# Attention part of a streaming encoder step: ScalarE and VectorE in written order, steps divided otherwise, weights split three chunks ahead

## The chip, the cores and the metric

One core of one Trainium2 chip runs the whole program. The metric is device time in microseconds (us) of one execution; the kernel before has a median of 2910.96 us over 3 runs (2910.06 to 2913.39).

## The reference, cut to what matters

One step of a two-layer encoder over 512 new frames ("prompt") and 8 running streams of 16 frames each ("sample"), 640 token columns in all; the model width is 2048.

```
# layer A
z = rmsnorm(x, norm_a) @ w_in_a ; u, gate = z[:4096], z[4096:]
x = x + (pool_mix(u) * silu(gate)) @ w_out_a
# shared keys, values, forget logits
kvf = rmsnorm(x, norm_kv) @ w_kv            # K 16 heads x 128, V 16 x 128, 16 logits
logf = log_sigmoid(kvf[..., 4096:] + b_f) ; F = cumsum(logf)
# layer B, 16 heads
z = rmsnorm(x, norm_b) @ w_in_b ; q, gate = z[:2048], z[2048:]
s = q.k / sqrt(128) + F[t] - F[s], causal   # sample streams also see 256 cached rows
o = softmax(s) @ v
x = x + (o * silu(gate)) @ w_out_b
y = rmsnorm(x, norm_f)
```

Everything is in float32. The kernel keeps the precision by splitting an operand into a rounded part (`hi`, type float32r, made on ScalarE) and the rest (`lo = x - hi`, made on VectorE), and by three matmuls for one product: hi*hi, hi*lo, lo*hi.

## The kernel before

**Layers A and K/V.** `pair8` multiplies a 256-column pair of weights by the stream with seven products of 2x2 blocks (m1 to m7, `ORDER`), each in a PSUM bank of its own (banks 0 to 6). `combine` (line 277) builds the four output blocks from them: first `v = m1` is copied out of PSUM by ScalarE (line 289), then VectorE adds and subtracts the others. The next pair's first matmul writes the same bank 0 again. It is called 47 times: 31 pairs of layer A, 16 of K/V. TensorE runs in the order in which the program is written; VectorE, ScalarE, GpSimd and the DMA queue on SyncE are ordered by a planner, which fills a list for each engine ahead of time. On the chip each engine works through its list in order and waits at each instruction for what that needs.

**Forget logits.** `forget_sums(c)` (line 782) adds, for each pair of stream blocks, small matmuls into banks 6 and 7. The last one, `forget_sums(7)`, runs in `last_rows` inside the first K/V pair, and both banks are then copied to `lt` (lines 865 and 866). Bank 7 is also the bank of `norm_stream`'s matmul (line 877), which comes three products later.

**Attention.** For each head `h`, `q_block(h)` and `gate_block(h)` each run `proj`: 16 k-steps of 6 matmuls (`mm3`, line 1069), in 4 chunks of 4 k-steps. At the start of a chunk `chunk()` calls `split_next` (line 1093): the weights of a later chunk are scaled on VectorE (line 1090), rounded on ScalarE (`whi`, line 1098), and the rest is taken on VectorE (`wlo`, line 1100); then `fetchb` asks for another chunk's DMA. `prime` splits two chunks in advance, and `whi` and `wlo` have three buffers each.

Between k-steps, at 9 of the 16 (k-steps 0, 2, 4, 6, 8, 9, 11, 13, 15), `tick()` runs one step of the generator `attn`, up to its next `yield`. In the steady state one head's attention steps are spread over `gate_block(h)` (9 ticks) and `q_block(h+1)` (9 ticks); it has 17 steps. The steps that matter here:

- steps 1, 2, 4, 5: `turn_keys`, VectorE transposes of cached keys into `kct` (line 1232);
- step 3 and step 7: `running`, matmuls of `kct` with the sample queries (line 1237);
- `new(t)`, t = 0 to 3 (steps 3, 6, 8, 9): scores of a 128-query block on TensorE; on VectorE add of F (line 1251), mask (1253), maximum (1255); on ScalarE Exp with a row sum (1257); on VectorE reciprocal (1258) and scaling (1259);
- step 7 also has the same chain for the sample rows, `s2` (lines 1305 to 1315);
- `turn_new(t)` (steps 8, 10, 11, 14): TensorE transposes of the probabilities into a bank from `tbank()`, which alternates between banks 6 and 7; ScalarE copies the rounded part out (`pth`, line 1269), VectorE takes the rest (`ptl`, line 1270);
- steps 12 and 13: transposes of `s2` (four blocks, then one) into the same two banks, copied out by ScalarE (line 1338);
- step 15 and 16: sample output `po` (line 1347); step 17: prompt output `op` (lines 1360 to 1363), ScalarE copies of both into `og`, VectorE product with the gate (line 1371).

After `q_block`'s last k-step VectorE makes `qt` and `qs` from PSUM (lines 1187 to 1190), ScalarE and VectorE split `qt`. After `gate_block`'s last k-step VectorE scales the gate (line 1199) and ScalarE applies Silu (line 1200). ScalarE loads a table whenever it goes from Exp to Silu or back.

**Output projection.** Planned freely on all engines, TensorE included, with `mmx` (line 1413).

## Time and profile before

| | |
|---|---|
| profiled execution | 2911.26 us, of which the span from the first to the last instruction is 2909.3 us |
| median of the runs | 2910.96 us |
| TensorE (PE) busy | 2780.2 us, 96% of the span |
| VectorE (DVE) busy | 2014.5 us, 69% |
| ScalarE (ACT) busy | 1149.5 us, 40% |
| GpSimd (POOL) busy | 382.2 us, 13% |
| layers A and K/V | from the start to about 1956 us |
| attention, 16 heads | about 1961 to 2680 us |
| output projection | from about 2663 us to the end |

TensorE is what the time is made of: where it runs without a gap, only fewer matmuls would help, and where it has gaps, the question is which instruction of another engine ended the gap. A row of the timeline has start, duration, engine, line, operation, output and inputs, and in brackets the idle time before it and what ended that. A row of the view of waits has the total, the number and the longest of such gaps.

### The profile page before, as it was taken

How to read it: one execution, taken by the hardware profiler on the slowest of the kernel's cores; microseconds unless marked ns; L12 is line 12 of the kernel's file. 1: busy time of each engine (PE TensorE's matmuls, PEld its weight loads, DVE VectorE, ACT ScalarE, POOL GpSimd, SP SyncE). 2: the span in 40 equal slices, each digit the busy share in tenths (PEclk: the TensorE clock that was granted, in tenths of full speed). 3: DMA queues.
4: the chain of work that ended last, by engine and by line, in shares of the span. 5: the costliest groups of instructions: out<-in, count | busy, mean ns of one | idle time of the engine just before them, and what ended most of it. 6: DMA issues, size and time to landing. Idle time of an engine off the chain costs nothing. (4 is left out here: it accounts for less than half of the span.)

```text
span 2909.3 us, 46312 instructions
## 1 busy us (share of the span) xinstructions
PE 2780.2 (96%) x18194; PEld 2651.2 (91%) x18194; DVE 2014.5 (69%) x3430; ACT 1149.5 (40%) x1911; POOL 382.2 (13%) x357
## 2 busy tenths in 40 slices
PE   7899999999999999999998999998999999999998
PEld 6799999999999999999998999987888888888787
DVE  7877778887786858584567888875665665656434
ACT  5433333333233435353345555542433433435222
POOL 2112131322420111112023111110000000000000
PEclk8999999999999999999999999999999999999999
DMA  3344444444345877779443554556555554545923
GB/s 124 114 130 134 132 124 129 128 131 125 112 130 164 200 166 182 171 180 182 139 145 89 117 127 117 121 123 152 138 129 128 134 131 118 133 126 110 144 85 110
DMA packets 646755, 390.69 MB, mean 134 GB/s; under 512 B 322756, under 2 KB 601716, under 8 KB 646408
## 3 DMA queue, kind: packets, MB, share of 16 engines
q1 hardware_dynamic: 626952, 333.99, 43.4%
q0 software_dynamic: 19584, 53.75, 8.6%
q8 instruction: 142, 2.33, 0.3%
q14 instruction: 77, 0.63, 0.1%
HBM read 299.66 MB, written 87.99 MB: 133 GB/s over the span
## 5 line engine op out<-in xcount | busy, mean ns | idle before, releaser
L251 PE MATMUL banks<-b,wh 128*128 128x320 f32 x2688 | 602.7, 311 | 16.7 <-ACT cve L289 10.6
L251 PE MATMUL banks<-th,wh 128*128 128x320 f32 x1792 | 566.9, 316 | 9.5 <-DVE cu L293 4.6
L251 PE MATMUL banks<-th,wl 128*128 128x320 f32 x1792 | 557.3, 311 | 2.8 <-DVE wl L84 2.8
L251 PE MATMUL banks<-tl,wh 128*128 128x320 f32 x1792 | 557.6, 311 | 0.7 <-DVE tl L84 0.7
L251 PEld LDWEIGHTS banks<-b,wh 128*128 128x128 f32 x2688 | 452.5, 189 | 18.3 <-ACT cve L289 11.6
L251 PE MATMUL banks<-b,wl 128*128 128x320 f32 x1344 | 417.2, 310 | 0.0
L84 DVE TENSOR_TENSOR wl<-raw,wh 128x768 fp32r<-128x768 f32 (+1 forms) x264 | 308.5, 1170 | 143.0 <-ACT wh L81 139.7
L81 ACT ACTIVATE wh<-sums 128x1024 fp32r<-128x1024 f32 x224 | 236.3, 1055 | 371.0 <-DVE sums L220 370.8
L81 ACT ACTIVATE wh<-raw 128x768 fp32r<-128x768 f32 (+1 forms) x264 | 230.2, 873 | 345.3 <-issue 154.8
L251 PEld LDWEIGHTS banks<-th,wh 128*128 128x128 f32 x1792 | 340.2, 190 | 19.8 <-DVE cu L293 9.1
L1069 PE MATMUL banks<-b,whi 128*128 128x320 f32 x1536 | 358.0, 317 | 0.0
L251 PEld LDWEIGHTS banks<-th,wl 128*128 128x128 f32 x1792 | 339.9, 190 | 3.3 <-DVE wl L84 3.3
L251 PEld LDWEIGHTS banks<-tl,wh 128*128 128x128 f32 x1792 | 340.2, 190 | 1.2 <-DVE tl L84 0.9
L84 DVE TENSOR_TENSOR wl<-sums,wh 128x1024 fp32r<-128x1024 f32 x224 | 282.1, 1259 | 70.6 <-ACT wh L81 70.0
L1069 PEld LDWEIGHTS banks<-b,whi 128*128 128x128 f32 x1536 | 257.8, 191 | 1.2 <-issue 0.4
L251 PEld LDWEIGHTS banks<-b,wl 128*128 128x128 f32 x1344 | 254.1, 189 | 0.0
L1069 PE MATMUL banks<-b,wlo 128*128 128x320 f32 x768 | 197.7, 312 | 0.0
L217 DVE TENSOR_TENSOR sums<-raw 128x512 f32<-128x512 f32 x236 | 174.9, 741 | 11.5 <-POOL sq L769 4.5
L1098 ACT ACTIVATE whi<-raw 128x512 fp32r<-128x512 f32 x144 | 88.9, 628 | 160.7 <-DVE raw L1090 89.8
L1100 DVE TENSOR_TENSOR wlo<-raw,whi 128x512 fp32r<-128x512 f32 x144 | 98.1, 687 | 72.6 <-ACT whi L1098 72.3
L213 ACT ACTIVATE raw<-raw,cols 128x256 f32<-128x256 f32 x256 | 111.1, 497 | 62.1 <-DMA raw<-in_w_kv 62.1
L1069 PEld LDWEIGHTS banks<-b,wlo 128*128 128x128 f32 x768 | 135.4, 190 | 0.0
(395 smaller groups left out, 4864.7 us busy)
## 6 DMA issues: line engine op xcount, KB each, us to landing
raw<-in_w_in_a SPq DMA_DIRECT2D x128, 512.0 KB, 4.0
raw<-in_w_out_a SPq DMA_DIRECT2D x64, 512.0 KB, 5.0
raw<-in_w_kv SPq DMA_DIRECT2D x64, 512.0 KB, 4.1
raw<-in_w_in_b SPq DMA_DIRECT2D x128, 256.0 KB, 3.9
raw<-in_w_grp_a SPq DMA_DIRECT2D x32, 512.0 KB, 5.6
kc<-in_cache_k SPq DMA_DIRECT2D x64, 256.0 KB, 5.3
vc<-in_cache_v SPq DMA_DIRECT2D x16, 1024.0 KB, 5.6
raw<-in_w_out_b SPq DMA_DIRECT2D x64, 256.0 KB, 3.3
```

The costliest lines, as they stand in the source:

```text
L81: a = nc.scalar.activation(hi, x, AF.Copy)
L84: nc.vector.tensor_tensor(lo, x, hi.bitcast(F32), op=ALU.subtract)
L213: nc.scalar.activation(raw[:, k, :], raw[:, k, :], AF.Copy, scale=loads[n][2][:, k : k + 1])
L217: nc.vector.tensor_tensor(sums[:, :, 0:2, :], raw[:, :, 1:3, :], raw[:, :, 0:1, :].to_broadcast([P, 2, 2, P]), op=ALU.subtract)
L251: nc.tensor.matmul(bank[:, :HALF], w[kk][:, a, :], x, start=first and q == 0, stop=last and q == 2)
L1069: nc.tensor.matmul(acc_[:, s, :HALF], w, stream(k, q, s), start=f, stop=l)
L1098: nc.scalar.activation(hi, raw, AF.Copy)
L1100: nc.vector.tensor_tensor(lo, raw, hi.bitcast(F32), op=ALU.subtract)
```

## The change

1. `combine`'s copy of the first product is done by VectorE instead of ScalarE (47 copies).
2. The partial forget logits of banks 6 and 7 are copied to `lt` before the K/V pairs; the last pair's matmuls go to bank 7, one half of the columns at product 2 and one at product 5 of the first K/V pair, and each half is added to `lt` by VectorE. `last_rows` is called at product 5 instead of 2.
3. `whi` and `wlo` have four buffers instead of three, and `prime` splits three chunks in advance. `prime` and the load of `R` stand ahead of the attention part's other loads.
4. From `prime` to the end of the attention part VectorE and ScalarE run in the order in which the program is written, as TensorE does, instead of the planner's.
5. The steps of `attn` are divided otherwise: the scaling of the probabilities (`even`) and the rest of their split (`low`) are taken out of `new` and `turn_new` and written one to three steps later; the values are split in step 8; the new keys of the next head two steps later; and there is one `yield` more, so that a head has 18 steps, one for each tick, and its last step (`op`, line 1360 on) now comes at the last k-step of `q_block`.

The diff, cut to its core:

```diff
         v, u, e = cvue
-        nc.scalar.activation(v, pp["m1"][:, :HALF], AF.Copy)
+        nc.vector.tensor_copy(v, pp["m1"][:, :HALF])
...
+    nc.scalar.activation(lt[:, :HALF], banks[:, 6, :HALF], AF.Copy)
+    nc.vector.tensor_copy(lt[:, HALF:], banks[:, 7, :HALF])
+    def last_forget(n):
+        hs = slice(n * HALF, (n + 1) * HALF)
+        for k in (14, 15):
+            q = k % 4
+            nc.tensor.matmul(banks[32 * q : 32 * q + 32, 7, :HALF], wr[0][:, k * H : k * H + 32], stage[7][:, k % 2, hs],
+                             start=True, stop=True)
+        nc.vector.tensor_tensor(lt[64:, hs], lt[64:, hs], banks[64:, 7, :HALF], op=ALU.add)
     def last_rows():
-        forget_sums(7)
-        nc.scalar.activation(lt[:, :HALF], banks[:, 6, :HALF], AF.Copy)
-        nc.vector.tensor_copy(lt[:, HALF:], banks[:, 7, :HALF])
...
-            if (n, s, j) == (0, 0, 2):
-                last_rows()
+            if (n, s) == (0, 0) and j in (2, 5):
+                last_forget(j // 3)
+                if j == 5:
+                    last_rows()
...
-            hi, lo = (wp.tile([P, 512], F32R, tag=q, name=q, bufs=3) for q in ("whi", "wlo"))
+            hi, lo = (wp.tile([P, 512], F32R, tag=q, name=q, bufs=4) for q in ("whi", "wlo"))
...
+        for _ in range(3):          # prime
+            split_next()
+            fetchb()
...
+    fast.enter_context(tc.manual_schedule(engines={mybir.EngineType.DVE, mybir.EngineType.Activation}))
+    prime()
...
                 nc.scalar.activation(s, s, AF.Exp, bias=mx, accum_out=rw)      # new(t)
-                nc.vector.reciprocal(rw, rw)
-                nc.vector.tensor_scalar_mul(s, s, rw)
+                rws[t] = rw
+            def even(t):
+                nc.vector.reciprocal(rws[t], rws[t])
+                nc.vector.tensor_scalar_mul(pr[t], pr[t], rws[t])
...
+            def low(t):
+                n = min(t + 1, 3)
+                ts = slice(t * P, (t + 1) * P)
+                nc.vector.tensor_tensor(ptl[:, :n, ts], turned[t], pth[:, :n, ts].bitcast(F32), op=ALU.subtract)
...
             turn_keys(kct, 1, 0)
+            even(0)
             yield
...
             running(ss, kct, 1)
+            even(1)                 # ahead of s2's chain
...
             yield
             new(2)
+            nc.vector.reciprocal(rw2, rw2)
+            nc.vector.tensor_scalar_mul(s2, s2, rw2)
+            split_new_values(h)
+            yield
             turn_new(0)
+            even(2)
             yield
+            low(0)
             new(3)
-                split_new_keys(h + 1)
             yield
             turn_new(1)
+            even(3)
+                split_new_keys(h + 1)
             yield
+            low(1)
             turn_new(2)
             yield
+            low(2)
             for js in ((0, 1, 2, 3), (4,)):
...
             turn_new(3)
             yield
+            low(3)
```

## The prediction

> **What bounds the kernel now.** I read the page first, then the time by stage, then TensorE's waits in the two parts that the change touches, then the timelines of VectorE and ScalarE inside one head.

> ```profile
> PE 2780.2 (96%) x18194; PEld 2651.2 (91%) x18194; DVE 2014.5 (69%) x3430; ACT 1149.5 (40%) x1911; POOL 382.2 (13%) x357
> ```
> ```profile
> 100.00:700.00 600.00, 591.81 (x4000) 588.57 (x4001) 481.28 (x776) 212.87 (x301) 137.14 (x150) 0.99 0.43 129
> ...
> 2059.84:2634.36 574.52, 530.67 (x3667) 484.20 (x3668) 349.52 (x768) 214.76 (x429) 0.00 (x0) 0.99 0.53 129
> ```

> TensorE is busy 96%, so only its gaps can be won or lost, 129 us in all. The second row (columns: length, then busy time of PE, weight load, DVE, ACT, POOL) spans 13 heads of the attention part: 574.52 / 13 = 44.19 us for a head. What TensorE waits for, first inside those 13 heads, then the same weight wait over the whole attention part, then in the parts before:

> ```profile
> PE banks L1069 <- ACT whi L1098: 24.5, 20, 1.5
> PE banks L105 <- DVE pr L1259: 19.3, 13, 2.0
> ```
> ```profile
> PE banks L1069 <- ACT whi L1098: 36.0, 23, 5.7
> ```
> ```profile
> PE banks L251 <- ACT cve L289: 10.6, 4, 3.0
> PE banks L251 <- DVE cu L293: 4.6, 2, 2.4
> ...
> PE banks L251 <- DVE cu L290: 3.3, 7, 1.8
> ...
> PE banks L877 <- DVE lt L866: 2.8, 1, 2.8
> ```

> In a head TensorE waits for rounded weights (24.5 / 13 = 1.9 us) and, at the transposes of block 2, for scaled probabilities (19.3 / 13 = 1.5 us): 3.4 us. That is all that the change can win there, 44 us in 13 heads; outside them the weights cost 36.0 - 24.5 = 11.5 more, 5.7 at the start and 5.8 in the first head. Before attention, the copy that it moves costs 10.6 us in four waits, and the bank of the forget logits 2.8 us.

> **Attention, VectorE and ScalarE in written order.** A head has 8 chunks, so three chunks ahead are 3 x 44.2 / 8 = 16 us, and I cost the weight waits at nothing. Their DMAs:

> ```profile
> raw<-in_w_in_b SPq DMA_DIRECT2D x128, 256.0 KB, 3.9
> ```
> ```profile
> SPq L1084 <- DVE wlo L1100: 242.2, 48, 10.7
> ```

> SyncE asks for a chunk when the rest of the fourth one before it is taken, as it did before (it stands and waits for that 242 us), and the data lands 3.9 us later, three chunks ahead of their use. The two stores of the values leave the queue's place behind the load that they wait for and go to step 8, where the values have long landed: nothing. If that cover is gone, the queue is a rival below.

> The question is what VectorE is late with next. The planner had mixed independent instructions so that VectorE never waited in the crowded part of a head:

> ```profile
> 2087.32:2098.33 11.01, 9.99 (x67) 9.56 (x68) 11.01 (x28) 6.74 (x14) 0.00 (x0) 1.00 0.98 190
> ```
> ```profile
> 2084.54 0.48 DVE L1251 SCALAR_TENSOR_TENSOR pr<-banks,Fs,fk 128x256 f32<-128x256 f32 x1 [0.42 <-PE banks L1249]
> 2085.06 0.29 DVE L1253 TENSOR_TENSOR pr<-pr,cm 128x128 f32<-128x128 f32 x1
> ...
> 2089.83 0.81 DVE L1311 TENSOR_REDUCE mx<-s 128x1 f32<-128x640 f32 x1
> 2090.56 0.68 DVE L1100 TENSOR_TENSOR wlo<-raw,whi 128x512 fp32r<-128x512 f32 x1
> ```
> ```profile
> L1258 DVE RECIPROCAL rw<-rw 128x1 f32<-128x1 f32 x52 | 8.1, 157 | 0.0
> ...
> L1315 DVE TENSOR_SCALAR s<-s,rw 128x640 f32<-128x640 f32 x13 | 7.1, 545 | 0.0
> ...
> L1259 DVE TENSOR_SCALAR pr<-pr,rw 128x256 f32<-128x256 f32 x13 | 4.5, 348 | 0.0
> ```

> VectorE is busy 11.01 of 11.01 us from the sample scores (line 1305) to `ptl` of block 1 (line 1270). In written order the same stretch ends with `low(1)`. It has one chunk's scale and rest more (0.61 us each) and one reciprocal and scaling less (0.16 and 0.35 in the rows below, each 0.08 less when the next follows at once, as 0.81 and 0.73 show): +0.9. Consecutive links of a chain now follow each other directly: a dependent instruction starts 0.52 us after one of 0.48, an independent one 0.73 after one of 0.81, so a dependent pair costs 0.12 more; nine pairs: +1.1. Then come waits for ScalarE, whose order is now fixed too:

> ```profile
> L1098 ACT ACTIVATE whi<-raw 128x512 fp32r<-128x512 f32 x104 | 63.7, 627 | 81.8 <-DVE raw L1090 63.2 <-PE banks L1069 12.2 <-DVE rw L1258 5.7
> L1257 ACT ACT_TABLE_LOAD x13 | 16.7, 1283 | 31.8 <-DVE mx L1255 31.7
> L1200 ACT ACT_TABLE_LOAD x13 | 16.7, 1283 | 0.2
> ...
> L1313 ACT ACTIVATE s<-s,mx 128x640 f32<-128x640 f32 x13 | 10.7, 823 | 2.1 <-DVE mx L1311 2.1
> ...
> L1200 ACT ACTIVATE sgb<-sgb 128x640 f32<-128x640 f32 x13 | 9.6, 739 | 0.1
> L1257 ACT ACTIVATE pr<-pr,mx 128x512 f32<-128x512 f32 x13 | 9.4, 722 | 8.4 <-DVE mx L1255 8.4
> ...
> L81 ACT ACTIVATE kh<-kt 128x512 fp32r<-128x512 f32 x13 | 8.1, 625 | 2.1 <-PE banks L1249 2.1
> L1257 ACT ACTIVATE pr<-pr,mx 128x384 f32<-128x384 f32 x13 | 8.0, 613 | 5.0 <-DVE mx L1255 5.0
> ...
> L81 ACT ACTIVATE vh<-vn 128x384 fp32r<-128x384 f32 x13 | 6.6, 507 | 0.0
> ```
> ```profile
> 2079.63 1.28 ACT L1257 ACT_TABLE_LOAD   x1 [4.53 <-DVE mx L1255]
> 2080.92 0.40 ACT L1257 ACTIVATE pr<-pr,mx 128x128 f32<-128x128 f32 x1
> ```

> Each number here is the ScalarE work since the last common point, less what VectorE still has to do meanwhile.
> - The rest of the chunk at k-step 12 waits for its `whi`, which stands behind the Exp of `s2`: 0.82 + 0.10 + 0.63 less one scale, 0.6: 1.0.
> - `vl` waits for `vh` behind the Exp of block 2: 0.61 + 0.10 + 0.51 less the reciprocal and scaling of `s2`, 0.16 + 0.55 with 0.1 of overlaps: 0.6.
> - The first chunk of the next `q_block` waits behind Silu and its table load: 1.28 + 0.74 + 0.63 - 0.1 less 0.6 (the scale hides a part): 2.1.
> - `even(3)` waits for the Exp of block 3, which now stands behind Silu, so that its table load starts only with the maximum (the load of 2079.63 did so too): 1.28 + 0.72 + 0.2: 2.2.
> - `kl` behind `kh`: 0.2.

> Sum 6.1. So `low(1)` ends 11.0 + 0.9 + 1.1 + 6.1 = 19.1 us after the sample scores begin. Behind it, on TensorE, stand the four transposes of `s2`: banks 6 and 7 alternate, block 1's transposes used the same bank, and `low(1)` must have read it (the transposes of block 2 wait for `low(0)` in the same way, a part of the same lateness). TensorE needs for that stretch:

> ```profile
> 2087.19 0.49 PE L1304 MATMUL banks<-kt,qs 128*128 128x128 f32 x2
> ...
> 2096.39 0.55 PE L105 MATMUL banks<-ident,pr 128*128 128x128 f32 x3 [1.02 <-DVE pr L1259]
> ...
> 2098.54 0.60 PE L105 MATMUL banks<-ident,s 128*128 128x128 f32 x4
> ```
> ```profile
> 2052.42 1.76 PE banks L1069 x12
> ```

> Before, from the sample scores to these transposes, 2098.54 - 2087.19 - 1.02 of waiting = 10.3 us with nine k-steps; now eleven, 0.88 each (12 matmuls are two): 12.1. TensorE is 19.1 - 12.1 = 7.0 us short in each head.

> A second wait comes at `running` (step 3). The head's last step now follows the last k-step, so VectorE reaches the new `qt` only behind `og`:

> ```profile
> 2068.53 0.27 PE L105 MATMUL banks<-ident,ob 128*128 128x128 f32 x1
> ```
> ```profile
> 2069.52 0.83 DVE L1371 TENSOR_TENSOR og<-og,sgb 128x640 f32<-128x640 f32 x1 [4.07 <-ACT og L1367]
> 2070.44 0.49 DVE L1187 SCALAR_TENSOR_TENSOR qt<-banks,R 128x320 f32<-128x320 f32 x1
> ...
> 2072.51 1.30 DVE L1232 STREAM_TRANSPOSE kct<-kc 128x512 f32<-128x512 f32 x2
> ```

> From the last transpose to `kct` 4.0 us; in written order one scale and one rest more (1.2), 0.2 less because `qt` no longer waits for TensorE: 5.0, and 0.7 for the transpose itself. TensorE gets there after five k-steps, 4.4: a wait of 1.3.

> So 8.3 us of waits replace 3.4 in a head: +4.9. The same reckoning, written out for the order that the trace shows, gives 44.5 for a head and 4.3 of waits where the trace has 44.2 and 3.4; I take the 0.9 off: +4.0, in 13 heads +52. The first head loses two waits for weights and gets the bank's, the last can be filled by output matmuls, which are not pinned: 0, bounds -6 and +6.

> [...]

> **The copy on VectorE.** 47 copies; VectorE's nearest row is the K/V copy of the same shape:

> ```profile
> 1544.03 0.48 DVE L866 COPY lt<-banks 128x320 f32<-128x320 f32 x1
> ```

> 47 x 0.48 = 23 us more on an engine that is 80% busy there (481 of 600), 0.5 us per pair, off TensorE's path unless it makes weights late. The 10.6 us go if VectorE reaches the copy sooner than ScalarE did; the planner draws its whole list anew. Bounds -10.6 and +10 (the waits for line 290 and 293 doubled); I take -6, nearer the row that names the copy.

> **Forget logits.** The 2.8 us wait goes. In its place `norm_stream` follows the second half's addition directly: its 0.48 and the hops, 0.7. -2, bounds -2.8 and +2.8 (VectorE as late as before). The order of `prime` and `R` I cost at nothing: TensorE's first attention matmul waits for `whi`, whose raw weights are still the first load; bounds -1 and +4 (a key transpose ahead of it).

> **Sum.** 52 + 0 - 6 - 2 = +44. The profiled execution took 2911.26 (span 2909.3 and 2.0 around it): 2955; the median of the runs is 0.3 lower: 2955.

> **Rivals.**
> - *The waits go and nothing takes their place* (faster). Weights ahead and written order leave VectorE no later than TensorE: 44 us in 13 heads, 6 in the first, 8 from copy and logits: 2853. It decides at `low(1)`: it must end within 12.1 us instead of 19.1. For it: VectorE is busy only 349.5 of 574.5 us. Against it: the 11.01 of 11.01. [...]
> - *The stalls shrink* (no change). If table loads are run ahead of their maximum (2.6 off) and most hops overlap (1.0), 4.7 of waits stay, 3.8 by the trace's scale: +0.4 a head, +5; with the copy and the logits at their best -13: 2903 to 2916.
> - *More is late.* Weights' DMAs queue behind blocked loads on SyncE: +4.9 a head at full size, +6 in the first, +10 from the copy: 2991.

> **Chances.** Forecast 0.70, stalls at full size or with more late 0.08, shrunk stalls 0.06 (all within or just around 0.2%, which is about what a measurement can tell from no change), waits simply gone 0.16. So slower 0.78, same 0.06, faster 0.16. Range 2908 to 2988: it leaves out the faster rival and the end of the slow one.

> **What would show it.** Right: gaps at line 105 ended by `ptl` line 1270 once or twice in every head, some 6 us together; a gap at line 1237 ended by `kct`; hardly any ended by `whi`; VectorE idle before line 1100 and line 1258 because of ScalarE; heads of 48 us. Copy: no gap ended by line 289's copy. Wrong: heads under 42 us, or ScalarE not in written order (Silu behind the Exp of block 3).

## The result and the profile after

The changed kernel takes 2988.18 us (median of 4 runs, 2986.05 to 2991.24) against 2912.18 beside it: ratio 1.0262, 95% interval 1.0244 to 1.028. Predicted were 2955 and 2908 to 2988; it is slower as forecast, by 76 us instead of 44, just past the end of the range. All profile rows and stretches below are of one profiled execution of each kernel. First the row of the page with the engines' busy time, then the thirteen heads that the prediction reckoned with (columns: length, TensorE busy, granted clock, DMA share, GB/s), then TensorE's waits inside them:

```profile
PE 2804.9 (94%) x18194; PEld 2679.0 (90%) x18194; DVE 2061.5 (69%) x3479; ACT 1129.1 (38%) x1864; POOL 376.0 (13%) x357
```
```profile
2082.97:2705.76 622.79, 548.75 (x3667) 0.96 0.48 119
```
```profile
PE banks L105 <- DVE ptl L1296: 59.8, 26, 3.3
PE banks L1253 <- DVE kct L1248: 14.2, 13, 1.1
```

The waits for `whi` and for scaled probabilities are gone, and the two that the prediction named stand in their place, in every head. But the same 3667 matmuls also take 548.75 us instead of 530.67, and the clock that TensorE was granted is 0.96 of full speed instead of 0.99. One head, TensorE's three gaps:

```profile
2241.33 1.64 PE L1253 MATMUL banks<-kct,qs 128*32 128x256 f32 x8 [1.09 <-DVE kct L1248]
...
2262.08 0.55 PE L105 MATMUL banks<-ident,pr 128*128 128x128 f32 x3 [1.30 <-DVE ptl L1296]
...
2267.69 0.65 PE L105 MATMUL banks<-ident,s 128*128 128x128 f32 x4 [3.30 <-DVE ptl L1296]
```

Where the 78.6 us of the two spans lie (marks: the attention part's first matmul, and each head's first sample-output matmul):

| stretch | before | after | planned order (e4, below) |
|---|---|---|---|
| to the attention's first matmul | 1961.3 | 1964.8 | 1961.4 |
| to head 0's output | 51.2 | 68.0 | 51.6 |
| head 0 to 1 | 47.3 | 50.2 | 46.3 |
| heads 1 to 14 (13) | 574.5 | 622.8 | 551.8 |
| head 14 to 15 | 39.4 | 44.6 | 36.6 |
| to the end | 235.6 | 237.5 | 236.4 |

### The profile page after: what moved, and what is told of

It is laid out like the page before. It is cut to its first block, busy times and chain, and to the rows that moved or that the text cites. A ratio compares the mean times of both kernels' runs of the same rounds, so it can differ in the third digit from the quotient of the medians.

```text
span 2987.9 us, 46409 instructions
## 1 busy us (share of the span) xinstructions
PE 2804.9 (94%) x18194; PEld 2679.0 (90%) x18194; DVE 2061.5 (69%) x3479; ACT 1129.1 (38%) x1864; POOL 376.0 (13%) x357
## 5 line engine op out<-in xcount | busy, mean ns | idle before, releaser
L251 PE MATMUL banks<-b,wh 128*128 128x320 f32 x2688 | 601.7, 310 | 18.9 <-DVE cve L289 12.4
L251 PE MATMUL banks<-th,wh 128*128 128x320 f32 x1792 | 565.5, 316 | 4.3 <-DVE cu L293 1.9
L251 PE MATMUL banks<-th,wl 128*128 128x320 f32 x1792 | 558.7, 312 | 3.1 <-DVE wl L84 3.1
L251 PE MATMUL banks<-tl,wh 128*128 128x320 f32 x1792 | 558.3, 312 | 0.5 <-DVE tl L84 0.5
L251 PEld LDWEIGHTS banks<-b,wh 128*128 128x128 f32 x2688 | 451.1, 189 | 21.8 <-ACT wh L81 6.5
L251 PE MATMUL banks<-b,wl 128*128 128x320 f32 x1344 | 416.9, 310 | 0.0
L81 ACT ACTIVATE wh<-sums 128x1024 fp32r<-128x1024 f32 x224 | 236.4, 1055 | 352.8 <-DVE sums L220 352.8
L1077 PE MATMUL banks<-b,whi 128*128 128x320 f32 x1536 | 368.1, 325 | 0.0
L81 ACT ACTIVATE wh<-raw 128x768 fp32r<-128x768 f32 (+1 forms) x264 | 230.3, 873 | 349.3 <-PE banks L251 145.9
L251 PEld LDWEIGHTS banks<-th,wh 128*128 128x128 f32 x1792 | 341.2, 190 | 10.3 <-DVE cu L293 4.2
L251 PEld LDWEIGHTS banks<-th,wl 128*128 128x128 f32 x1792 | 340.6, 190 | 3.6 <-DVE wl L84 3.6
L251 PEld LDWEIGHTS banks<-tl,wh 128*128 128x128 f32 x1792 | 341.1, 190 | 1.1 <-DVE tl L84 1.0
L1077 PEld LDWEIGHTS banks<-b,whi 128*128 128x128 f32 x1536 | 268.8, 198 | 1.9 <-issue 0.2
L251 PEld LDWEIGHTS banks<-b,wl 128*128 128x128 f32 x1344 | 253.5, 189 | 0.0
L217 DVE TENSOR_TENSOR sums<-raw 128x512 f32<-128x512 f32 x236 | 176.5, 748 | 12.1 <-POOL sq L769 4.5
L666 PE MATMUL banks<-th,wh 128*128 128x320 f32 x576 | 132.1, 310 | 1.6 <-DVE cu L290 1.1
## 6 DMA issues: line engine op xcount, KB each, us to landing
raw<-in_w_in_b SPq DMA_DIRECT2D x128, 256.0 KB, 2.9
kc<-in_cache_k SPq DMA_DIRECT2D x64, 256.0 KB, 4.8
raw<-in_w_out_b SPq DMA_DIRECT2D x64, 256.0 KB, 3.3
```

The lines of the kernel that those rows point to most:

```text
L81: a = nc.scalar.activation(hi, x, AF.Copy)
L217: nc.vector.tensor_tensor(sums[:, :, 0:2, :], raw[:, :, 1:3, :], raw[:, :, 0:1, :].to_broadcast([P, 2, 2, P]), op=ALU.subtract)
L251: nc.tensor.matmul(bank[:, :HALF], w[kk][:, a, :], x, start=first and q == 0, stop=last and q == 2)
L666: nc.tensor.matmul(bk[s], w, x[:, s * HALF : (s + 1) * HALF], start=k + q == 0, stop=k == 7 and q == 2)
L1077: nc.tensor.matmul(acc_[:, s, :HALF], w, stream(k, q, s), start=f, stop=l)
```

## The experiments

Each run stands as median and ratio to the kernel before on the same chip, with its 95% interval. The recorded expectations name what they weigh against each other theory A and rival (B or D). "A head" is a thirteenth of the stretch from head 1 to 14.

**One part at a time, on the kernel before (e1, e2, e3), and the written order alone taken away (e4).**

```diff
-        nc.scalar.activation(v, pp["m1"][:, :HALF], AF.Copy)     # e1
+        nc.vector.tensor_copy(v, pp["m1"][:, :HALF])
```

> The kernel before with one edit: the copy of the first product (line 289) on VectorE. The step of the prediction says -6 us (between -10.6, the four waits of TensorE for ScalarE's copy gone, and +10). Rival, read from the trace of after: the four waits shrink to about 1.9 each and five new ones of about 1.0 appear in the layers K and V, so the waits sum to 12.4 instead of 10.6 and the edit is worth +0 to +4. Told apart by the sum of TensorE's waits at line 251 and by the start of the attention's first matmul (1961.4 before): 1955 by the prediction, 1961 to 1965 by the rival.

2911.58 us, 0.9998 (0.9989 to 1.0007): nothing, which fits the rival. The first line is of the kernel after, the second of e1:

```profile
PE banks L251 <- DVE cve L289: 12.4, 9, 1.9
```
```profile
PE banks L251 <- DVE cve L289: 16.6, 11, 3.5
```

The four waits of before (10.6 us) became nine and eleven: TensorE now waits for VectorE's copy instead of ScalarE's.

> The kernel before with one edit: the last two chunks of the forget gate's product in last_forget, behind the splits of chunk 7, and the logits' copies ahead of it. The prediction says -2 us (between -2.8, the wait at line 877 gone, and +2.8). Rival, read from the trace of after: the copy on VectorE stands behind the sums of squares that wait for GpSimd, so TensorE's wait of 2.79 us is replaced by one of 4.74 and one of 0.71, and the edit is worth about +2.5.

e2 takes `last_forget` over as the change's diff shows it: 2912.53 us, 0.9997 (0.9985 to 1.0009). The wait of 2.8 us at bank 7 went, and one of 6.3 came, for the copy ahead of it. The interval, about -4 to +3 us, holds the predicted -2 as well as the rival's +2.5, so the run does not tell them apart.

```profile
PE banks L869 <- DVE lt L863: 6.3, 1, 6.3
```

> The kernel before with one edit: four buffers instead of three for the two halves of the split weights, and three chunks split ahead of the first head. Theory A (the change's heads lose because of the written order, and the wait for the weights' halves, 1.9 us per head before, is made by the number of buffers): the waits shrink to about 0 and the heads get shorter by up to 1.9 us each, 13 x 1.9 = -25 us, 2887. Rival B: the wait is made by the place that the splits have in VectorE's list, with buffers to spare: no change, 2908 to 2916.

e3 (`bufs=4`, three splits in `prime`): 2903.03 us, 0.9966 (0.9953 to 0.9979). Theory A in kind, under half of it in size (11 us of 25). In the thirteen heads no wait for `whi` is left; these stand instead, and a head is 43.2:

```profile
PE banks L105 <- DVE pr L1258: 17.4, 13, 1.4
PE banks L105 <- DVE ptl L1269: 13.5, 13, 1.0
PE banks L1246 <- DVE s L1304: 6.3, 13, 0.5
```

```diff
-    fast.enter_context(tc.manual_schedule(engines={mybir.EngineType.DVE, mybir.EngineType.Activation}))   # e4
```

> The kernel after with one edit: the line that makes ScalarE and VectorE take the attention part in written order is gone, so that the order of these two engines is planned again as in the kernel before; the divided steps, the three chunks ahead, the copy and the logits stay as in the kernel after. Theory A (the written order makes the three new waits of a head, 5.7 us each): head to head goes back from 47.95 to 44.2 or below, the first head loses its wait of 10.9 us at the queries' scaling, and the time is 2880 to 2920. Rival B (the division of the steps, or the weights' fourth buffer, makes the waits): the waits for the turned scores (3.3) and for the turned keys (1.1) stay and the time is 2960 or more.

2884.77 us, 0.9909 (0.9893 to 0.9925): the kernel after without its one line is 103 us faster than with it, and 0.9% faster than the kernel before. The table's last column shows that the line costs in every stretch of the attention part: 71 us in thirteen heads, 16 in the first, 8 in the last.

**Which engine's order (e5, e6), and with which steps (e9).** The line names VectorE alone in e5, ScalarE alone in e6; e9 is e3 with the line, so the old steps in written order.

> The kernel after with the written order on VectorE alone; ScalarE's order is planned. The written order on both costs 103 us against the planned one (2988 against 2885). Theory A (VectorE's written order holds the heads back: the scores' splits ahead of the next copies of turned scores, and the weights' low halves between them): 2960 to 2990, head to head 46.5 to 48. Rival B (ScalarE's order does it: the gate's Silu and its two table loads stand between the copies of turned scores, and VectorE only waits for ScalarE): 2885 to 2910, head to head 43 to 44.5.

> The other half: the kernel after with the written order on ScalarE alone; VectorE's order is planned. Theory A (VectorE's order): 2885 to 2910. Rival B (ScalarE's order): 2945 or more.

> The kernel before with four buffers and three chunks ahead (as the run with that edit alone, 2903 us), and its undivided steps in written order on ScalarE and VectorE in the attention part. It is the fourth corner of a square: planned order and old steps 2903, planned order and divided steps 2885, written order and divided steps 2988. Theory A (the two add up: the written order costs some 100 us with any steps, the divided steps are worth some 18): about 3006 (2990 to 3030). Rival B (the divided steps, as written, are what places the low halves badly; the old ones have the low half right behind its copy): 2940 or less, head to head under 46.

e5: 2982.91, 1.0235 (1.0218 to 1.0252). e6: 2901.95, 0.9962 (0.9947 to 0.9977). Both fall where theory A put them: VectorE's order costs some 98 us, ScalarE's alone some 17. e9: 3070.27, 1.053 (1.0514 to 1.0546): outside both expectations, above theory A's sum and far from the rival. So the divided steps are worth 18 us in planned order (2903 to 2885) and 82 in written order (3070 to 2988), and the order costs 103 to 167 us depending on the steps. The two parts of the change do not add up; each has its price only beside the other.

**Moving steps in the written order (e7, e8, e10 to e14, e18).**

```diff
             turn_new(0)
+            low(0)                                              # e8
             even(2)
             yield
-            low(0)
...
             turn_new(1)
+            low(1)                                              # e8
...
             turn_new(3)
             yield
+                nc.scalar.activation(gates[-1], gates[-1], AF.Silu)   # e7: next head's gate
```

> The kernel after, both engines in written order, with one step moved on ScalarE: the Silu of the next head's gate stands behind the last copy and exponential of the head (after turn_new(3)) instead of between the steps of the old keys. By hand reckoning from the rows of after the head then takes 45.5 instead of 48.9: the wait for the turned scores' split of 3.3 us stays, those of 1.3 and 1.1 us shrink: 13 x -3.4 = -44, about 2944 (Theory C: the two table loads around Silu, 1.3 us each, lie on the chain of the head). Rival D: the chain of the head is VectorE's own amount of work between the waits, 19.1 us against 12.1 on TensorE, and the move changes little: 2980 to 2990.

> The kernel after with two steps moved on VectorE: the weights' low halves low(0) and low(1), 1.0 us each, stand right behind turn_new(0) and turn_new(1) instead of a step later, ahead of the copies that give back the ring of banks. By hand reckoning from the rows of after: head to head 47.2 instead of 48.9, the wait of 1.3 us at the second group of transposes goes, that of 3.3 grows to 5: 13 x -1.6 = -21, about 2967 (the prediction's reading that low(0) and low(1) lie in the chain of the bank ring). Rival: the low halves lie beside ScalarE's work and only change places: 2980 to 2995.

e7: 2972.71, 1.0202 (1.0185 to 1.0219): -15, between the two and nearer rival D, so the table loads around Silu are a small part of the chain. e8: 2946.45, 1.0112 (1.0097 to 1.0127): -42, twice what was expected. Its thirteen heads:

```profile
2074.20:2661.30 587.10, 537.32 (x3668) 0.98 0.51 126
```

TensorE's idle time fell from 74.0 (622.79 - 548.75) to 49.8, 1.9 a head, near the reckoned 1.6; the rest of what these heads won, 11.4, is matmuls that run faster. That opened the question of the clock (e17).

> The kernel with low(0) and low(1) early (2946 us), and besides the two transposes of head 0's keys moved behind the wait for its queries, so that they no longer stand on VectorE ahead of the first chunks' scales while their load is under way. Theory A (these transposes make TensorE's waits of 4.3 and 10.9 us in the first head): from the attention's first product to the first head's output 66 becomes 52 to 55, in all -9 to -14, 2932 to 2937. Rival B (the first head waits for its loads in any order): 2944 to 2949. The later heads don't change in either.

> The kernel with the four moves in the written order (2929 us), and besides head 0's loads of new keys, sums, values and new values put on SyncE behind the loads of the next four chunks of weights, one ahead of each (before: all of them ahead of the eighth chunk's load). Moving the transposes alone did nothing for the first head; VectorE then stood 17.6 us at the scale of the eighth chunk, whose load was issued at 1983.3, behind them. Theory A (the order of the loads on SyncE, with VectorE's list that can't pass the scale): the wait for the turned keys of 16.0 us ends some 12 us earlier, from the attention's first product to the first head's output 67 becomes 53 to 57, 2915 to 2919. Rival B (the loads are late in any order, the 16 queues being full): 2925 to 2932.

e10 (head 0's two transposes moved behind its queries): 2953.24, 1.0127 (1.0112 to 1.0142), no gain, the theory fell. Where VectorE now stands in the first head, and the load that it waits for:

```profile
1983.30 1.24 SPq L1092 DMA_DIRECT2D raw<-in_w_in_b  x1
...
1988.53 0.69 DVE L1098 TENSOR_TENSOR raw<-raw,cols 128x512 f32<-128x512 f32 x1 [17.57 <-DMA raw<-in_w_in_b]
```

VectorE stands 17.57 us at the scale of the eighth chunk, whose load SyncE issues behind all of head 0's loads; the queries wait behind that scale. e13 puts those loads, all but the cached keys', behind the weights', one in each of four chunks:

```profile
1975.56 1.52 SPq L1092 DMA_DIRECT2D raw<-in_w_in_b  x1
...
1980.79 0.69 DVE L1098 TENSOR_TENSOR raw<-raw,cols 128x512 f32<-128x512 f32 x1 [7.98 <-DMA raw<-in_w_in_b]
```

It stands on e12 (all four moves), whose first head took 66.9; e13's takes 56.6, as theory A said: 2920.78, 1.0022 (1.0013 to 1.0031) after e12's 2929.1, 1.0047 (1.0032 to 1.0063), so the time lies just above theory A's 2915 to 2919. The order of the loads was changed only together with the moved transposes, not alone.

> The kernel with low(0) and low(1) early (2946 us), and besides the second transposition of the second half of the keys one step earlier, right behind the first. Theory A (TensorE's wait of 1.1 us a head for the turned keys is this transposition's place behind a wait for the weights' high half): the wait goes, 13 x -1.1 = -14 at most, 2932 to 2940. Rival B (VectorE's list is full there, what goes ahead makes the scores late instead): 2943 to 2950.

> All four moves in the written order together: low(0) and low(1) early, head 0's keys behind its queries, the second transposition of keys earlier, Silu late. If they add up: 2946 - 12 (first head) - 14 (keys) - 15 (Silu, as measured alone) = 2905; head to head 42.8 to 43.5, the planned order's 42.4 nearly reached. Rival: each move only hands the time on to the next wait of the ring of banks, and 2920 to 2940 is left; the part of the written order that no move explains is then as large as that.

> The kernel of the run above, and besides the first transposition of a head's keys ahead of the gate's first split of weights (one step of the attention part is taken before the gate's product begins). The wait of 1.09 us a head that the earlier run left alone stands at the first of the two products with the keys, not at the second, so it is this transposition, behind one scale and one low half (0.69 us each) in VectorE's list, that is late. Theory A: the wait goes, 13 x -1.1 = -14 against the run above, head to head 42.8. Rival B: the low half that is now behind the transposition is late instead, a wait for the weights' halves of some 0.5 to 1 us appears: 0 to -7.

> The kernel with the first transposition of a head's keys ahead of the gate's first split of weights (2919 us), and the second with it. There the wait of 1.09 us only changed hands: the product with the keys began 0.9 us earlier and stopped 0.71 us for the second transposition, which stood where it was, and from the last matmul of the queries' product to the next block's scores it was 2.66 us in both. Theory A: with both transpositions ahead the wait is gone, 13 x -1.1 = -14, 2903 to 2909, head to head 42.8. Rival B: the weights' low half, now behind two transpositions (1.3 us), is what TensorE waits for: 2915 to 2922.

e11 (the second half's transposition one step earlier) changed nothing: 2949.18, 1.0112 (1.0096 to 1.0127), for the wait of 1.09 is at the first half's product. e12's 2929 is the rival's (2920 to 2940 left over): its moves do not add up. e14, on e13, moved the first of its two transposes: 2919.31, 1.0021 (1.001 to 1.0032), a gain no larger than the rival's, but not by the wait that the rival named. The wait changed hands inside the product:

```profile
2253.97 1.05 PE L1256 MATMUL banks<-kct,qs 128*32 128x256 f32 x4
2255.72 1.05 PE L1256 MATMUL banks<-kct,qs 128*32 128x256 f32 x4 [0.71 <-DVE kct L1251]
```

e18 moved both: 2900.97, 0.9959 (0.9946 to 0.9972), a head 42.9 instead of 43.9, theory A, and a little more than it said. In its heads only one kind of wait is left:

```profile
PE banks L105 <- DVE ptl L1299: 28.6, 25, 1.8
```

So the written order can be had for less than the kernel before, by moving `low`, Silu, the keys' transposes and the first loads; the planned order still is 16 us better.

**A wait filled with work (e17).**

```diff
+            for _ in range(8 if more else 0):
+                nc.tensor.matmul(banks[:, mmring.places[mmring.n % 2], :P], ident, R[:, :P], start=True, stop=True)
             for js in ((0, 1, 2, 3), (4,)):      # transposes of s2
```

> The kernel after, and in 15 heads eight matmuls of 128x128 (float32, the identity by a part of R, into banks that nothing reads then) on TensorE right ahead of the transposes of the sample scores, where it waits 3.30 us for VectorE. They take some 8 x 0.24 = 1.9 us of the wait and lie on nobody's path; no other instruction moves. Theory A (after this wait TensorE's granted clock stands at half for 3.4 us in 12 of 13 heads, which costs 1.71 us each time; waits of up to 1.7 us left it at 1.00): the idle time becomes some 1.4 us, the clock stays at 1.00, and the kernel gets faster by adding work: 13 x -1.7 = -22, about 2966, head to head 46.2 to 46.4. Rival B (the clock falls for another reason, the total load for one): the time stays at 2985 to 2995, or grows by what the eight matmuls take beyond the wait.

2963.38 us, 1.0171 (1.0156 to 1.0186): 25 us faster than the kernel after by 120 useless matmuls (each is two records in the trace). Below, the stretch around the 3.30 us wait of the kernel after (columns as in the first row of this kind):

```profile
2264.00:2266.00 2.00, 0.39 (x3) 1.00 0.48 163
2266.00:2268.00 2.00, 0.31 (x3) 1.00 0.21 38
2268.00:2270.00 2.00, 2.00 (x12) 0.62 0.53 154
2270.00:2272.00 2.00, 2.00 (x10) 0.53 0.05 13
```

Then the same place and the thirteen heads of e17:

```profile
2255.43 1.95 PE L1374 MATMUL banks<-R,ident 128*128 128x128 f32 x16
...
2258.89 0.66 PE L105 MATMUL banks<-ident,s 128*128 128x128 f32 x4 [1.51 <-DVE ptl L1296]
```
```profile
2078.70:2682.30 603.60, 552.64 (x3876) 1.00 0.50 122
```

The clock goes to half for 3.4 us after the long wait, and stays at 1.00 where the wait is cut to 1.51. A head is 46.4 instead of 47.9: theory A. The eight matmuls take 25.3 us in the thirteen heads; without them TensorE is busy 527.3 us there instead of 548.75, so the same matmuls ran 21 us faster.

**The planned order again (e15, e16).**

> The kernel after without the written order (2885 us), with low(0), low(1) and the second transposition of keys early as in the written kernels. If the planned order follows the program's text where it can, the remaining waits of TensorE for the scores (18.8 and 8.9 us in sum) shrink: 2865 to 2882. Rival: the planner places these instructions by itself, where they stand in the text hardly matters: 2880 to 2890.

> The kernel after without the written order (2885 us), and with the first product's copy back on ScalarE and the logits as in the kernel before: the divided steps and the three chunks ahead alone. The two edits alone moved nothing that could be measured (ratios 0.9998 and 0.9997): then 2882 to 2888. By the prediction's terms for them (-6 and -2) it would be 2893.

e15 (e4 with e8's and e11's moves): 2924.47, 1.0034 (1.002 to 1.0048). Outside both expectations: what won 42 us in written order lost 40 in planned order. The planner put the scaling of the probabilities later, in each of the thirteen heads (13 waits, the longest 3.8 us), and the mean clock there is 0.95, where it is 0.98 in e4:

```profile
PE banks L105 <- DVE pr L1277: 48.9, 13, 3.8
```
```profile
2056.80:2648.70 591.90, 543.04 (x3667) 0.95 0.51 126
```

Why it did so with only three instructions of a head moved stays open, and which of the two moves did it was not tried apart. e16 (e4 with the copy and the logits of the kernel before): 2885.44, 0.9904 (0.9886 to 0.9922), no different from e4. Both beat both kernels; the gain is the divided steps and the fourth buffer with the third chunk ahead.

## Why the prediction was right or wrong

**Heads: the sum right by luck, its parts not.** Predicted +4.0 a head, measured +3.7 (48.3 / 13). But idle time grew by 2.3 (74.0 less 574.52 - 530.67 = 43.9, by 13) and the slower matmuls added 1.4 (548.75 - 530.67, by 13). The prediction held that only TensorE's gaps can be won or lost, so it had no such term: a wait that was too large in it stood in for the clock. The mis-sized term is the bank wait: 7.0 predicted, 59.8 / 13 = 4.6 measured. Its chain, 19.1 us from the sample scores to the end of `low(1)`, is 16.7 in the trace, and 16.7 less the predicted 12.1 of TensorE is the measured 4.6:

```profile
2250.96 0.75 DVE L1336 SCALAR_TENSOR_TENSOR s<-banks,Fs,fs 128x512 f32<-128x512 f32 x1 [0.30 <-PE banks L1253]
...
2254.66 0.69 DVE L1108 TENSOR_TENSOR wlo<-raw,whi 128x512 fp32r<-128x512 f32 x1 [0.91 <-ACT whi L1106]
...
2257.99 0.56 DVE L84 TENSOR_TENSOR vl<-vn,vh 128x384 fp32r<-128x384 f32 x1 [0.53 <-ACT vh L81]
...
2261.13 0.69 DVE L1108 TENSOR_TENSOR wlo<-raw,whi 128x512 fp32r<-128x512 f32 x1 [0.73 <-ACT whi L1106]
...
2264.62 0.16 DVE L1277 RECIPROCAL rw<-rw 128x1 f32<-128x1 f32 x1 [0.88 <-ACT pr L1273]
...
2267.22 0.88 DVE L1296 TENSOR_TENSOR ptl<-banks,pth 128x256 fp32r<-128x256 f32 x2
```

Of the five stalls, 1.0 and 0.6 came out (0.91, 0.53); 2.1 (its own terms add up to 1.95) and 2.2 are 0.73 and 0.88, and 0.2 is none: 3.1 instead of 6.1, while the rest of the chain took 0.6 more. The step that failed: "its table load starts only with the maximum". It ran ahead of it, and Silu's ran ahead of its input:

```profile
2258.13 1.28 ACT L1216 ACT_TABLE_LOAD   x1
2259.84 0.74 ACT L1216 ACTIVATE sgb<-sgb 128x640 f32<-128x640 f32 x1 [0.43 <-DVE sgb L1215]
...
2261.12 1.28 ACT L1273 ACT_TABLE_LOAD   x1
2263.77 0.72 ACT L1273 ACTIVATE pr<-pr,mx 128x512 f32<-128x512 f32 x1 [1.37 <-DVE mx L1271]
```

That is what the rival "the stalls shrink" said, and e7 bears it out: Silu's place is worth 15 us, not the 44 expected there. The load of 2079.63, from which the prediction read its rule, did stand for the maximum, as 7 of the 13 loads of the Exp did there, and with Silu late, in e7, all 13 do so again. The traces tell the two kinds apart: right ahead of a load that stood, ScalarE's list has a row EVENT_SEMAPHORE of the load's own line. Below are the rows of these instructions (ACTq: instructions that only order others; the count, then ns and us), 7 in the kernel before and 13 in e7, and one such load of e7:

```profile
L1257 ACTq EVENT_SEMAPHORE  x7: 17/17/17, 2079.6 to 2609.8; - x7
```
```profile
L1274 ACTq EVENT_SEMAPHORE  x13: 17/17/17, 2096.3 to 2656.7; - x13
```
```profile
2281.78 1.28 ACT L1274 ACT_TABLE_LOAD   x1 [3.71 <-DVE mx L1272]
```

In the thirteen heads of the kernel after none stands ahead of a load; there the activation waits instead (0.43 and 1.37 us in the rows above), behind its load's end. The wait for `kct` was right in place and size (1.3 predicted, 1.09 measured); e18 shows its cause, the keys' transposes behind a scale and a rest.

**The weights' waits, costed at nothing.** e3 bears that out: with a fourth buffer and a third chunk ahead no wait for `whi` is left in the heads. The time won was 11 us, far from what the rival with all waits gone had for the heads (44), for VectorE was late with the next thing: in the heads 24.5 us of waits went and 17.9 came. Faster matmuls gave as much as the waits did: TensorE was busy 524.4 us there instead of 530.67, at a mean clock of 1.00 instead of 0.99, with no stretch at half clock instead of three.

**First head, predicted 0 (-6 to +6): the step that failed by most.** "The first head loses two waits for weights and gets the bank's": it lost 16.8 us to its first output and 2.9 to the next. The prediction reckoned with buffers and the bank ring, and not with the list: a planned VectorE takes the queries first, a written one stops at the first load that is not there. In planned order (e4):

```profile
1977.23 0.49 DVE L1202 SCALAR_TENSOR_TENSOR qt<-banks,R 128x320 f32<-128x320 f32 x1 [2.26 <-PE banks L1077]
...
1979.29 1.30 DVE L1247 STREAM_TRANSPOSE kct<-kc 128x512 f32<-128x512 f32 x2
```

In the kernel after the queries come only at 1996.29, behind these:

```profile
1982.97 1.30 DVE L1248 STREAM_TRANSPOSE kct<-kc 128x512 f32<-128x512 f32 x2 [12.99 <-DMA kc<-in_cache_k]
...
1995.08 0.69 DVE L1098 TENSOR_TENSOR raw<-raw,cols 128x512 f32<-128x512 f32 x1 [8.42 <-DMA raw<-in_w_in_b]
```

Taking the first of these away alone won nothing (e10): VectorE then stood 17.57 us at the second instead of 8.42, and the turned keys came behind it. With the second one's load ahead of head 0's other loads as well (e13) the head won 10 us; some 5 are left, and VectorE still stands 7.98 us there. The rival "more is late" named this queue, though not this place.

**Copy -6 and logits -2.** The -6 is ruled out: e1's interval, about -3 to +2 us, lies in the middle of the bounds and not near the row that names the copy. Gaps ended by line 289's copy, which were to vanish, are nine. For the logits no gain is shown (e2, and e16 against e4 for both edits), nor is -2 ruled out. The 0.7 us behind the second half's addition came out (0.7), but the step had no term for the copy ahead of it, at which TensorE waits 4.7 us in the kernel after:

```profile
PE banks L869 <- DVE lt L863: 4.7, 1, 4.7
```

**To the attention's first matmul** +3.4 instead of -8: for the 3.4 no cause is shown, and over the traces of the other kernels this mark lies anywhere between 1959.1 and 1966.5.

**Last head**, predicted 0: +5.2, and +1.9 to the end; in planned order -2.8 and +0.8. The written order costs there too, so the step "can be filled by output matmuls" failed: they did not cover it.

The miss, 34.6 us on the spans (78.6 less 44): first head 20 (with the stretch to the next output), last and end 7, before attention 11 (8 not won, 3 lost), less 4 in the heads.

## What to carry to other kernels

An engine's written order is priced by its own list: look for each instruction that waits for a slow producer (a load above all) and for what stands behind it that others need; the same few moves were worth -42 us in a written list and +40 in a planned one. A wait that is removed is only won where nothing else is late at the same place, so read what ends the next gap before counting it (e1, e3, e14). And read the granted clock behind a TensorE wait before counting the sum of the waits: in the kernel after 3.41 us at half clock went with each wait of 3.30 in the thirteen heads, and filling a part of it with work, 1.51 left, won 25 us (e17).

## What the runs showed of the hardware

```profile
2340.00:2342.00 2.00, 0.00 (x0) 0.99 0.14 42
2342.00:2344.00 2.00, 1.02 (x5) 0.50 0.17 44
2344.00:2346.00 2.00, 2.00 (x9) 0.50 0.46 132
2346.00:2348.00 2.00, 2.00 (x9) 0.50 0.40 118
2348.00:2350.00 2.00, 2.00 (x14) 0.80 0.00 0
```

The slow stretches of one trace began whole multiples of 3.413 us apart: in the thirteen heads 88.75 us (26 times that) in the kernel before, where they began at 2315.74, 2404.49 and 2493.24, and 47.78 us (14 times) from head to head in the kernel after; among those of e4 there are 85.32 (25 times) and among those of e8 44.38 (13 times). Two waits of nearly one length in the kernel before came out differently. Below, in steps of 3.41 us counted from these beginnings, are the two around a wait of 2.03 us and the two around one of 2.04 (columns: length, TensorE busy, granted clock, DMA share, GB/s):

```profile
2223.58:2227.00 3.42, 1.75 (x12) 1.00 0.94 187
2227.00:2230.41 3.41, 3.05 (x23) 1.00 0.34 81
2312.33:2315.74 3.41, 1.37 (x11) 1.00 0.85 203
2315.74:2319.15 3.41, 3.41 (x16) 0.50 0.21 54
```

In the thirteen heads of the kernel before, three steps at full clock were followed by a slow one, with TensorE busy 1.37 to 1.44 us in each; in the 161 that were followed by one at full clock it had been busy 1.75 us or more. In the kernel after they are 13, with 0.11 to 1.27 us, and 156, with 2.10 us or more. Between 1.44 and 1.75 these two traces have no step at full clock, and why the clock fell they do not say.

**Table loads.** In the kernel after, the two table loads of a head ran ahead of the input of the activation that needs them in all thirteen heads, and the activations began 0.4 and 1.4 us after their loads (1.28 us each) had ended. Elsewhere they did not: the load ahead of the first Exp of a head stood for the maximum 4.53 us in seven of thirteen heads of the kernel before, and 3.71 us in the row of e7 above. In the attention parts of the kernels before and after, 9 of 62 loads stood for more than 0.2 us, each right behind a semaphore instruction of its own line; the 53 without one stood 0.02 us or less, and in 29 of these cases the activation behind the load stood instead. Why the program has that instruction at one place and not at another stays open.
